# The first half of a merge gate by seven products, with v computed early and gates parked in DRAM

## The chip, the cores and the metric

The kernel runs on one core of one Trainium2 chip, in one launch. The metric is the device time of one execution in microseconds (us). The kernel before was run three times: 893.97, 894.41 and 895.62 us, median 894.41.

The engines go by these names: PE multiplies matrices (PEld is its weight load), DVE and ACT work on tiles elementwise, POOL and SP here issue transfers (DMAs) and do little else. Weights come from DRAM (also called HBM); SBUF is the on-chip memory for operands, PSUM the one that PE writes to.

## The reference

One encoder block over 256 tokens of width 2048. All inputs of the two branches, their gates and the two merge gates come out of one projection `z`; `m_lru` and `m_attn` are the merge gates' 2048 columns each.

```python
xn = rms_norm(x, norm_pre_w[l])
z = xn @ w_in[l]
u_lru, g_lru, q, k, v, g_attn, m_lru, m_attn = jnp.split(z, split_at, axis=-1)
u = centred_depthwise_conv(u_lru, conv_w[l], conv_b[l])
h = rg_lru(u, ..., False) + rg_lru(u, ..., True)
y_a = h.astype(x.dtype) * jax.nn.silu(g_lru)
...
y_b = windowed_gqa(q, k, v, attn_sink[l]) * jax.nn.silu(g_attn)
merged = (jax.nn.sigmoid(m_lru) * (y_a @ w_proj_a[l])
          + jax.nn.sigmoid(m_attn) * (y_b @ w_proj_b[l]))
x = x + rms_norm(merged @ w_out[l], norm_post_w[l])
```

## The kernel before

**Weights.** Every weight matrix is read in cells of 1 MB (128 x 2048 float32), in the order that `load_plan` writes down; two fetches of half a MB make up some of them. A cell's two halves are split by `split` (L231, L233) into a high part `wh` (rounded by ACT's cast) and a low part `wl` (what is left, by DVE), and PE forms each product from three matrix products: high by high, low by high, high by low (`mm3`, L237 to L239; L262 and L264 do the same with the two parts of the activation side by side). There are three kinds of cells. A "blk" gives 128 output columns with the weights as the stationary side (`add_pair`: the gates `gl` and `ga`, the recurrent inputs `u`, the keys `k`, the queries `q`). A "quad" is a quarter of 512 output columns with tokens as the stationary side (`add_rows`: `ml`, `v_ps`, `pa`, `ma`, `pb`, `o`); four quads make a chunk. A "part" is half of one of seven products (below).

**Seven products.** Half of a merge gate (1024 columns) can be had from seven products of half-size blocks in place of eight, in `Seven`: two token blocks by two halves of the inner dimension by two column halves of 512. The products m1 to m7 use sums of weight blocks and of activation blocks. The weight sums are formed by the transfers: a block is loaded by SP (`start`), and others are added to it in SBUF by accumulating DMAs that POOL issues (`load` with `add`, L204). The activation sums are formed by DVE (`x_sums`), stored to DRAM by SP (`away`) and fetched back a half product at a time (`x_sum`, L349). Each product has two parts, of 12 matmuls each, where a quad has 24. The results are put together by DVE (`combine`, L756) from PSUM and copies that ACT made (`keep`, L425). Before the change `Seven("L")` computes columns 1024 to 2047 of `m_lru`, `Seven("A")` the same columns of `m_attn`, and `Seven("O")` half of the output projection. Columns 0 to 1023 of `m_lru` are two chunks of quads, `ml0` and `ml1`, by `add_ml`.

**Order of the work.** The emission loop at the end of `body` walks over the cells in ticks. A tick is one half of a blk or quad, or a whole part: 12 matmuls of 512 columns, or 8 of 512 and 8 of 256. In each tick the loop issues a fetch three cells ahead (sums and chained loads four and five ahead), runs the closures due at that tick, has ACT cast the weights four halves ahead and DVE form the low part three halves ahead, and then emits PE's matmuls. Every engine works through its own queue in this order. Closures are put at a tick by `at`, `soon` and `behind`: the recurrence of a pair of blocks (`lru_pair`, from tick `LRU[c]`), the heads of attention, the evacuations of PSUM. The program has 298 ticks. The first 142, up to v's last, are:

- `u` quads (ticks 0 to 7), `ml0` (8 to 15), then gl, ga and u pairs, `ml1` at ticks 40 to 47, and between the blks from tick 56 to 121 the 14 parts of `L`, one after every second blk (`EARLY_L`);
- the keys, and v's four quads at ticks 134 to 141.

Then `MERGE` takes over: queries and the projections `pa` in turn, the gate `m_attn` with its seven products, `pb`, and at last the output projection.

**Buffers.** Tiles of 4 KB a partition come from one pool of 45 (`unit`); raw cells go through a ring of three; PSUM has four single banks (`bank`) and two double ones. Of the values that wait long, the chunks 0 and 1 of the merge gate and the products `pa` of chunks 2 and 3 are stored to DRAM by `park` (L780) and fetched by `back` (L783), all on SP's queue. The silu gates `sgl` and `sga` stay in SBUF, and `ya`, the recurrent branch's result in two parts, is made as soon as a pair's recurrence ends (`y_parts`).

Of the kernel before, what the change touches and what calls it, by code (L numbers as in the profile page):

```python
# [27 lines left out]
ROT = 32  # L28
EPS = 1e-6
UNITS = 45  # L30
EARLY = (0, 2)
DECAY = 12
SPIN = 10
HEAD0 = 5
FIRST = 8
ROWS = 10
U0, GL0, Q0, K0, V0, GA0, ML0, MA0 = 0, 2048, 4096, 6144, 6656, 7168, 9216, 11264
# [28 lines left out]
CHUNKS = {"p": ("w_proj_a", 0), "a": ("w_in", MA0), "b": ("w_proj_b", 0), "o": ("w_out", 0)}  # L66
SEVENS = {"L": ("w_in", ML0 + 1024), "A": ("w_in", MA0 + 1024), "O": ("w_out", 0)}


PV_NORM = 0  # L70
# [9 lines left out]
def load_plan():  # L80

    plan = []

    def quad(m, c):
        plan.extend(("quad", m, c, i) for i in range(4))

    def pair(m, c, n):
        plan.extend(("blk", m, c + (n + i) * P, 0) for i in range(2))

    quad("w_in", U0)  # L90
    for i in range(8):
        if i in EARLY:
            quad("w_in", ML0 + EARLY.index(i) * 512)
        for j, c in enumerate([GL0 + 2 * i * P, GA0 + 2 * i * P] + [U0 + (2 * i + 4) * P] * (i < 6)):
            for n in range(2):
                plan.append(("blk", "w_in", c + n * P, 0))
                if (i, 2 * j + n) in EARLY_L:
                    a, q = EARLY_L[i, 2 * j + n].split(".")
                    plan.append(("part", "L", a, int(q)))
    pair("w_in", K0, 0)  # L100
    pair("w_in", K0, 2)
    quad("w_in", V0)
    for o in MERGE + OUT:
        a, i = o.split(".")
        if a[0] in SEVENS:
            plan.append(("part", a[0], a[1:], int(i)))
        elif a[0] == "q":
            plan.append(("blk", "w_in", Q0 + (4 * int(a[1]) + int(i)) * P, 0))
        else:
            w, c = CHUNKS[a[0]]  # L110
            plan.append(("quad", w, c + int(a[1]) * 512, int(i)))
    return plan


# [13 lines left out]
def body(ctx, tc, x, xT, wall, wlru, pvec, npost, ident_d, mask_d, rope_d, out):  # L128
# [442 lines left out]
    for g in range(4):  # L571
        steps.append(("quad", lambda h, wh, wl, g=g: u_quad(g, h, wh, wl)))

    upads = {}

# [58 lines left out]
    def lru_pair(n, b):  # L634
# [69 lines left out]
        def gate_out():  # L704
# [13 lines left out]
        for d, fn in (  # L718
            (0, lambda: conv(0)), (1, lambda: conv(1)), (2, weights), (3, u_parts),
            (6, lambda: gates(0)), (7, lambda: sigmoids(0)), (8, lambda: gates(1)), (9, lambda: sigmoids(1)),  # L720
            (10, lambda: decays("th", AF.Tanh, cpos, 0)), (10, lambda: decays("th", AF.Tanh, cpos, 1)), (11, gated),
            (12, lambda: decays("a", AF.Exp, cneg, 0)), (13, lambda: decays("a", AF.Exp, cneg, 1)),
            (13, lambda: nc.scalar.activation(v["gr"], v["a"], AF.Square)), (14, scale1),
            (15, lambda: nc.scalar.activation(v["th"], v["th"], AF.Sqrt)),
            (19, lambda: nc.vector.tensor_tensor(v["gi"], v["gi"], v["th"], ALU.mult)),
            (21, lambda: scans(0)), (24, lambda: scans(1)), (28, gate_out), (29, y_parts),
        ):
            at(b + d, fn)

    def silu_evac(units_list, n):  # L730
# [16 lines left out]
    def gate_unit(gates, c):  # L747
        if c not in gates:
            gates[c] = unit(f"mg{c}", F32, (P, 2, 512))
        return gates[c]  # L750

    def gate_evac(gates, c):
        return lambda t, ps: nc.scalar.activation(gate_unit(gates, c)[:, t], ps, AF.Sigmoid, scale=rtok[:, t:t + 1])

    def combine(to, ps, other, sign):
        nc.vector.scalar_tensor_tensor(to, ps, float(sign), other, ALU.mult, ALU.add if sign > 0 else ALU.subtract)  # L756

    def gate_sum(gates):

        def done(t, c, ps, other, sign):  # L760
            to = gate_unit(gates, 2 + c)[:, t]
            gate = lambda src: nc.scalar.activation(to, src, AF.Sigmoid, scale=rtok[:, t:t + 1])
# [12 lines left out]
    parked = {}  # L775

    def park(gates, c):

        d = parked[c] = dram.tile([P, 1024], F32, name=f"park{c}")
        nc.sync.dma_start(d, flat(gates.pop(c)))  # L780

    def back(gates, c):
        nc.sync.dma_start(flat(gate_unit(gates, c)), parked[c])  # L783
# [9 lines left out]
    for c in range(8):  # L793
        if c in EARLY:
            add_ml(EARLY.index(c))
        first_step = len(steps)
        add_pair(f"gl{2 * c}", xs, silu_evac(sgl, 2 * c))
        add_pair(f"ga{2 * c}", xs, silu_evac(sga, 2 * c))
        if c < 6:
            n = 2 * c + 4  # L800
            add_pair(f"u{n}", xs, lambda ps, n=n: scaled(upad_tile(n)[:, :, 2:2 + S], ps))
        mine = steps[first_step:]
        del steps[first_step:]
        for j, s in enumerate(mine):
            steps.append(s)
            if (c, j) in EARLY_L:
                a, q = EARLY_L[c, j].split(".")
                groups["L"].add(a, int(q))
        lru_pair(2 * c, LRU[c])


    swap = [(i + 16) % 32 for i in range(32)]
# [5 lines left out]
        nc.sync.dma_start(table["mask"], mask_d)  # L818
        nc.sync.dma_start(table["rope"], rope_d)

    at(ticks() - 6, load_tables)

    def add_heads(name, then):

# [27 lines left out]
                then(v["h"], v["l"])  # L852
                v.clear()

        for n in (0, 2):
            add_pair(f"{name}{n}", xs, evac(n))

    kv = {}
    add_heads("k", lambda h, l: kv.update(kh=h, kl=l))

    def v_evac(t, ps):
        if t == 0:
            kv["vh"], kv["vl"] = (unit(f"v{s}", F32R, (P, 2, 512)) for s in "hl")
        vh, vl = kv["vh"][:, t], kv["vl"][:, t]
        nc.scalar.activation(vh, ps, AF.Copy, scale=rtok[:, t:t + 1])
        soon(lambda: nc.vector.scalar_tensor_tensor(vl, ps, rtok[:, t:t + 1], vh.bitcast(F32), ALU.mult, ALU.subtract))

    add_rows("v_ps", xs, v_evac)

    def head(hd, qh, ql, b, both):  # L870

# [50 lines left out]
        def gate_out():  # L922
            y = sga[g][:, j - 1:j + 1]
            nc.vector.tensor_tensor(y, both["o"], y, ALU.mult)
            both.clear()

        for d, fn in ((0, scores), (1, expo), (3, normalise), (5, flip), (6, p_parts)):
            at(b + d, fn)
# [9 lines left out]
    def heads(g):  # L938
        def then(h, l):
            b = now[0] + HEAD0  # L940
            for j in range(4):
                if j % 2 == 0:
                    both = {}
                head(4 * g + j, h, l, b + 4 * j, both)
        return then


    def add_pa(c):
        def done(t, ps):
            nc.vector.tensor_tensor(tm[c][:, t], ps, tm[c][:, t], ALU.mult)  # L950
            if t == 1 and c >= 2:
                soon(lambda: park(tm, c), 2)

        add_rows(f"pa{c}_", ya, done)

# [23 lines left out]
    def add_all(order, classic):  # L979
        left, tick = {}, {}  # L980
        for o in order:
            a, i = o.split(".")
            tick[o] = ticks()
            if a[0] in SEVENS:
                groups[a[0]].add(a[1:], int(i))
                continue
            if i == "0":
                n = len(steps)
                classic(a[0], int(a[1]))
# [6 lines left out]
    tick = add_all(MERGE, lambda kind, c: {  # L996
        "q": lambda: add_heads(f"q{c}", heads(c)),
        "p": lambda: add_pa(c),
        "a": lambda: add_rows(f"ma{c}_", xs, gate_evac(sm, c)),
        "b": lambda: add_pb(c),  # L1000
    }[kind]())
    for c in range(4):
# [182 lines left out]
```

## Time and profile before

| what | value |
|---|---|
| median of three runs | 894.41 us |
| span of the profiled execution | 892.7 us |
| PE busy | 883.7 us (99%), 4590 matmuls |
| DVE busy | 698.5 us (78%), 959 instructions |
| ACT busy | 600.4 us (67%), 870 instructions |
| POOL busy | 44.8 us (5%), 72 instructions |
| DMA | 209.95 MB, mean 235 GB/s |
| HBM read, written | 200.78 MB, 8.39 MB |

The profiled execution's own time is its span of 892.7 us plus what lies around it; the median of the runs is 1.7 us above the span. Busy time is the union of an engine's instructions. Matmuls overlap in the pipeline and their ends are modelled, so that what a matmul costs in a saturated stream is the distance from its start to the next one's start, not its duration.

### The profile page before, as it was taken

Reading aid. Unit: us, or ns where it says so; the run is one execution under the profiler, and the core shown is the slowest. Engines: PE = TensorE matmul, PEld = TensorE weight load, DVE = VectorE, ACT = ScalarE, POOL = GpSimd, SP = SyncE. Lnnn points to the kernel's source line nnn. Section 1 sums busy time; section 2 is a strip of 40 time slices with the busy share of each in tenths; the row PEclk is TensorE's granted clock in tenths of the full one; section 3 lists DMA queues with packets and bytes.
Section 4 is the critical chain, followed back from the end, with each engine's and each line's share of the span. In section 5 each row is a group of like instructions: output and inputs, shape, how many; then the busy total and the mean of one; then the engine's idle time right before and its main releaser. Section 6 shows DMA issues by size and latency. Waiting matters only on the chain.

```text
span 892.7 us, 12161 instructions
## 1 busy us (share of the span) xinstructions
PE 883.7 (99%) x4590; PEld 758.2 (85%) x4590; DVE 698.5 (78%) x959; ACT 600.4 (67%) x870; POOL 44.8 (5%) x72
## 2 busy tenths in 40 slices
PE   9999999999999999999999999999999999999996
PEld 8888888888888888888888888888888888888885
DVE  6897999788888989899757767676676776687775
ACT  7689686787878788885454565455587654455754
POOL 0000000000110100000000000000101100000200
PEclk9999999999999999999999999999999999999998
DMA  9766667897797946365555444546979987799962
GB/s 337 260 224 237 211 226 281 245 297 280 242 303 259 276 172 217 107 230 198 211 185 213 162 168 145 209 146 239 280 253 310 286 258 256 278 325 378 232 177 95
DMA packets 43642, 209.95 MB, mean 235 GB/s; under 512 B 4512, under 2 KB 9376, under 8 KB 26560
## 3 DMA queue, kind: packets, MB, share of 16 engines
q1 hardware_dynamic: 36096, 183.25, 56.2%
q0 software_dynamic: 6912, 25.17, 14.9%
q8 instruction: 36, 0.59, 0.3%
q10 hardware_dynamic: 576, 0.76, 0.2%
q14 instruction: 22, 0.18, 0.1%
HBM read 200.78 MB, written 8.39 MB: 234 GB/s over the span
## 4 chain that ended last, share of the span: by engine, by line
PE 93%; issue 4%; DMA 2%; DVE 0%; POOLq 0%; ACTq 0%; POOL 0%; DVEq 0%
PE q L264 7%; PE gl L264 7%; PE ga L264 7%; PE u L264 5%; PE ga L262 3%; PE gl L262 3%; PE q L262 3%; PE u L262 3%; PE k L264 2%; PE Am L237 1%; PE Am L239 1%; PE Am L238 1%; PE Lm L239 1%; PE Lm L238 1%; PE Lm L237 1%
## 5 line engine op out<-in xcount | busy, mean ns | idle before, releaser
L233 DVE TENSOR_TENSOR wl<-raw,wh 128x1024 fp32r<-128x1024 f32 (+1 forms) x276 | 326.8, 1203 | 63.8 <-ACT wh L231 43.4
L231 ACT CAST wh<-raw 128x1024 fp32r<-128x1024 f32 (+1 forms) x275 | 275.8, 1040 | 43.5 <-DMA raw<-wall_dram 24.4
L264 PE MATMUL q<-xs,wh 128*128 128x512 f32 x256 | 62.8, 391 | 0.0
L264 PE MATMUL ga<-xs,wh 128*128 128x512 f32 x256 | 62.6, 391 | 0.0
L264 PE MATMUL gl<-xs,wh 128*128 128x512 f32 x256 | 62.6, 391 | 0.0
L264 PEld LDWEIGHTS ga<-xs,wh 128*128 128x128 f32 x256 | 46.9, 188 | 9.0
L264 PEld LDWEIGHTS gl<-xs,wh 128*128 128x128 f32 x256 | 46.9, 188 | 9.0
L264 PEld LDWEIGHTS q<-xs,wh 128*128 128x128 f32 x256 | 46.6, 188 | 8.8
L264 PE MATMUL u<-xs,wh 128*128 128x512 f32 x192 | 46.9, 391 | 0.0
L160 ACT CAST ph<-pt 128x512 fp32r<-128x512 f32 x16 | 9.4, 588 | 55.3 <-PE pt L908 55.3
L264 PEld LDWEIGHTS u<-xs,wh 128*128 128x128 f32 x192 | 35.0, 188 | 6.6
L262 PE MATMUL q<-xs,wl 128*128 128x256 f32 x256 | 34.4, 284 | 0.0
L262 PEld LDWEIGHTS ga<-xs,wl 128*128 128x128 f32 x256 | 33.2, 191 | 1.3
L262 PEld LDWEIGHTS q<-xs,wl 128*128 128x128 f32 x256 | 33.1, 191 | 1.2
L262 PE MATMUL ga<-xs,wl 128*128 128x256 f32 x256 | 34.0, 283 | 0.0
L262 PEld LDWEIGHTS gl<-xs,wl 128*128 128x128 f32 x256 | 32.9, 191 | 1.2
L262 PE MATMUL gl<-xs,wl 128*128 128x256 f32 x256 | 33.4, 283 | 0.0
L888 DVE CUSTOM_DVE_ANT_0 p<-sc,table,pv 128x256 f32<-128x256 f32 x32 | 16.1, 541 | 13.4 <-PE sc L239 13.4
L262 PEld LDWEIGHTS u<-xs,wl 128*128 128x128 f32 x192 | 24.6, 191 | 0.9
L262 PE MATMUL u<-xs,wl 128*128 128x256 f32 x192 | 24.9, 283 | 0.0
L658 DVE SCALAR_TENSOR_TENSOR uu<-upad,pv,uu 128x256 f32<-128x256 f32 x48 | 23.2, 483 | 2.2 <-ACT uu L654 0.5
L681 ACT ACTIVATE gr<-gate,pv 128x256 f32<-128x256 f32 x32 | 15.2, 476 | 11.7 <-PE gate L239 11.7
(493 smaller groups left out, 2188.5 us busy)
## 6 DMA issues: line engine op xcount, KB each, us to landing
raw<-wall_dram SPq DMA_DIRECT2D x133, 1024.0 KB, 5.8
lraw<-wlru_dram SPq DMA_DIRECT2D x8, 512.0 KB, 7.0
away<-xx SPq DMA_DIRECT2D x8, 512.0 KB, 4.5
Lm<-away SPq DMA_DIRECT2D x8, 512.0 KB, 7.9
Am<-away SPq DMA_DIRECT2D x8, 512.0 KB, 8.0
raw<-wall_dram SPq DMA_DIRECT2D x8, 256.0 KB, 5.2
park<-mg SPq DMA_DIRECT2D x4, 512.0 KB, 6.1
mg<-park SPq DMA_DIRECT2D x4, 512.0 KB, 6.2
```

Source lines behind the costliest of these rows:

```text
L160: nc.scalar.copy(h, src)
L231: cast(hs, raw)
L233: nc.vector.tensor_tensor(ls, raw, hs.bitcast(F32), ALU.subtract)
L237: nc.tensor.matmul(ps, wh, xh, start=start, stop=False, skip_group_check=more)
L238: nc.tensor.matmul(ps, wh, xl, start=False, stop=False, skip_group_check=more)
L239: nc.tensor.matmul(ps, wl, xh, start=False, stop=stop, skip_group_check=more)
L262: nc.tensor.matmul(ps[:, 1], wl[:, sl], a[:, 0], start=False, stop=False)
L264: nc.tensor.matmul(ps, wh[:, sl], a, start=k == 0, stop=k == KT - 1)
L658: nc.vector.scalar_tensor_tensor(u, up[:, j, tap:tap + S], cw[:, tap:tap + 1], u, ALU.mult, ALU.add)
L681: nc.scalar.activation(v["gr"][:, 2 * d + j], ps[:, 0], AF.Sigmoid, bias=pv[:, PV_BR + b:PV_BR + b + 1])
L888: nc.vector.tensor_tensor_reduce(p[:, t], sc[:, t], table["mask"][:, t], rtok_sc[:, t:t + 1], sk, ALU.add, ALU.max, m[:, t:t + 1])
```

## The change

The two chunks `ml0` and `ml1` are gone. A further object `Seven("M")` computes columns 0 to 1023 of `m_lru` by seven products, its 14 parts standing behind those of `L`. v's four quads take the place of `ml0` right after `u`; the keys stand at the end, between M's last parts. The order up to the keys is now written out in a table, `START`, which `load_plan` and `add_all` both read. The parts of `L` begin earlier, at tick 44, one behind each blk for the most part, those of M follow from tick 92 to 137; the eight `x_sums` stand every four ticks from tick 18 on, where they stood every five from 20. The pairs' recurrences start at ticks 12, 28, 42, 58, 75, 92, 109 and 122, where they started at 12, 28, 45, 64, 79, 94, 109 and 121. The program has 296 ticks; `p0.0`, the first projection cell, is at tick 148 in place of 150.

More values are kept in DRAM: the gates `sgl` (three of four tiles, once multiplied with the recurrence's result), `sga` (all four tiles, and three of them again once multiplied with the attention's result), all four chunks of the gate, and all four products `pa`. That makes 18 parks and 18 returns of 512 KB each, where there were four and four. Six of the eight `ya` are therefore formed later, in ticks 145 to 151, from the fetched tiles.

The core of the diff:

```diff
-EARLY = (0, 2)
...
-EARLY_L = {(2, 3): "m1.0", (2, 5): "m1.1", (3, 1): "m2.0", (3, 3): "m2.1", (3, 5): "m5.0", (4, 1): "m5.1", (4, 3): "m3.0",
-           (4, 5): "m3.1", (5, 1): "m6.0", (5, 3): "m6.1", (5, 5): "m7.0", (6, 1): "m7.1", (6, 3): "m4.0", (7, 1): "m4.1"}
-XSUM = (20, 25, 30, 35, 40, 45, 50, 55)
-LRU = (12, 28, 45, 64, 79, 94, 109, 121)
...
+START = """u0.0 u0.1 u0.2 u0.3 v0.0 v0.1 v0.2 v0.3 g0.0 g0.1 h0.0 h0.1 w4.0 w4.1 g2.0 g2.1 h2.0 h2.1 w6.0 w6.1 g4.0 g4.1
...
+XSUM = (18, 22, 26, 30, 34, 38, 42, 46)
+LRU = (-4, 0, 2, 2, 2, 2, 2, 4)
...
+SEVENS = {"L": ("w_in", ML0 + 1024), "M": ("w_in", ML0), "A": ("w_in", MA0 + 1024), "O": ("w_out", 0)}
...
-        def y_parts():
-            q = n // 2
-            ya[q] = pair_unit(f"ya{q}")
-            parts_of(ya[q][:, :, 0], ya[q][:, :, 1], sgl[n // 4][:, n % 4:n % 4 + 2])
+            if n in (2, 6, 10):
+                soon(lambda: park("ya", sgl, n // 4), 2)
+            elif n > 10:
+                soon(lambda: y_parts(n // 2))
...
+                if units_list is sga and n % 4 == 2:
+                    soon(lambda: park("sga", sga, n // 4), 3)
...
     Seven("L", xs, None, gate_sum(tm))
+    Seven("M", xs, None, gate_sum(tm, 0))
...
-    def add_ml(c):
-        def done(t, ps):
-            gate_evac(tm, c)(t, ps)
-            if t == 1:
-                soon(lambda: park(tm, c), 2)
-
-        add_rows(f"ml{c}_", xs, done, c == 0)
...
+    def park(key, store, c):
+
+        d = parked[key, c] = dram.tile([P, 1024], F32, name=f"park{key}{c}")
+        t = store[c]
+        store[c] = None
+        nc.sync.dma_start(d, flat(t))
+
+    def back(key, store, c, shape=(P, 2, 512)):
+        store[c] = unit(f"{key}{c}", F32, shape)
+        nc.sync.dma_start(flat(store[c]), parked[key, c])
...
     for c in range(4):
-        at(tick[f"p{c}.0" if c < 2 else f"b{c}.0"], lambda c=c: back(tm, c))
+        at(tick[f"p{c}.0"], lambda c=c: back("tm", tm, c))
+        at(tick[f"b{c}.0"], lambda c=c: back("pa", tm, c))
+    for c in range(4):
+        if c < 3:
+            at(tick["p0.0"] - 8 + 2 * c, lambda c=c: back("ya", sgl, c, (P, 4, S)))
+            at(tick["b0.0"] - 12 + 3 * c, lambda c=c: back("yb", sga, c, (P, 4, S)))
     for n in range(8):
-        at(tick["b0.0"] - 4 + 3 * n // 2, lambda n=n: yb_parts(n))
+        if n < 6:
+            at(tick["p0.0"] - 3 + n, lambda n=n: y_parts(n))
+        at(tick["b0.0"] - 6 + 3 * n // 2, lambda n=n: yb_parts(n))
```

In `START` g and h stand for pairs of the gates `gl` and `ga`, w for pairs of `u`, and `Lm1.0` for the first part of L's product m1. Its M stretch, from the first part to the last of M, reads: `Mm1.0 g10.1 Mm1.1 h10.0 h10.1 Mm2.0 w14.0 Mm2.1 w14.1 Mm5.0 g12.0 Mm5.1 g12.1 Mm3.0 h12.0 h12.1 Mm3.1 g14.0 Mm6.0 g14.1 Mm6.1 h14.0 Mm7.0 h14.1 Mm7.1 k0.0 k0.1 Mm4.0 k2.0 Mm4.1`.

**Three places in the order.** First PE, where `u` ends and the next chunk begins (tick 8). Before, the first chunk of the gate:

```order
L554 MATMUL u_ps_195<-xs_263,wh_1_290 128x512 x2
L554 MATMUL u_ps_196<-xs_263,wh_1_290 128x512 x2
L237 MATMUL ml_0_409<-wh_0_315,xs_124 128x512
L238 MATMUL ml_0_409<-wl_0_316,xs_124 128x512
L239 MATMUL ml_0_409<-wh_0_315,xs_124 128x512
```

After, v stands there with the same shapes, and the gate's columns come on PE as parts between two halves of a blk (tick 92, the first of them):

```order
L250 MATMUL gl_2784<-xs_258,wh_1_2725 128x512 x2
L250 MATMUL gl_2784<-xs_263,wh_1_2725 128x512 x2
L223 MATMUL Mm_2831<-wh_0_2756,xs_124 128x512
L224 MATMUL Mm_2831<-wl_0_2757,xs_124 128x512
L225 MATMUL Mm_2831<-wh_0_2756,xs_124 128x512
L223 MATMUL Mm_2831<-wh_0_2756,xs_135 128x512
```

What moved: 192 matmuls of `ml` are replaced by 168 of `Mm`, and v's 96 stand 126 ticks earlier.

Second DVE, just before the first `pa` chunk, where the first queries' rotation (`q0f`, `q0s`), the last recurrence (`gr`) and the low parts of weights (`wl`) are in the queue. Before:

```order
L589 TENSOR_TENSOR q0f_4229<-q_4144,q0f_4229 128x512
L233 TENSOR_TENSOR wl_0_4232<-raw_4183,wh_0_4231 128x1024
L841 STREAM_SHUFFLE q0s_4275<-q0f_4229 32x512
L842 TENSOR_TENSOR q0f_4229<-q0f_4229,table 32x512
L233 TENSOR_TENSOR wl_1_4254<-raw_4183,wh_1_4253 128x1024
L707 TENSOR_TENSOR gr_3794<-gr_3794 128x512
L708 TENSOR_TENSOR sg_3301<-gr_3794,sg_3301 128x512
L845 TENSOR_TENSOR q0s_4275<-q0s_4275,table 32x512
L846 TENSOR_TENSOR q0f_4229<-q0f_4229,q0s_4275 32x512
L233 TENSOR_TENSOR wl_0_4279<-raw_4227,wh_0_4278 128x1024
L233 TENSOR_TENSOR wl_1_4303<-raw_4227,wh_1_4302 128x1024
L161 TENSOR_TENSOR ya_4324<-sg_3301,ya_4324 128x2x256
```

After (`ya_4195` and `ya_4247` on the right of an arrow are the tiles fetched from DRAM):

```order
L147 TENSOR_TENSOR ya_4324<-ya_4195,ya_4324 128x2x256
L219 TENSOR_TENSOR wl_1_4329<-raw_4245,wh_1_4328 128x1024
L826 TENSOR_TENSOR q0s_4354<-q0s_4354,table 32x512
L827 TENSOR_TENSOR q0f_4301<-q0f_4301,q0s_4354 32x512
L147 TENSOR_TENSOR ya_4352<-ya_4195,ya_4352 128x2x256
L219 TENSOR_TENSOR wl_0_4359<-raw_4296,wh_0_4358 128x1024
L147 TENSOR_TENSOR ya_4378<-ya_4247,ya_4378 128x2x256
L219 TENSOR_TENSOR wl_1_4384<-raw_4296,wh_1_4383 128x1024
L147 TENSOR_TENSOR ya_4407<-ya_4247,ya_4407 128x2x256
L147 TENSOR_TENSOR q0l<-q0f_4301,q0h 128x512
L576 TENSOR_TENSOR q0f_4413<-q_4307,q0f_4413 128x512
L219 TENSOR_TENSOR wl_0_4416<-raw_4348,wh_0_4415 128x1024
```

What moved: six `ya`, which stood singly between ticks 42 and 124, now stand one in each tick ahead of the chunk that reads them, the low part two ticks ahead of PE's use.

Third SP, where it fetches for the last third of the recurrences' weights (`lraw`; `raw` is a cell, `Lm` an activation sum). Before:

```order
L219 DMA raw_2678<-wall_dram 128x2048
L349 DMA Lm_2680<-away_74 128x1024
L640 DMA lraw_2710<-wlru_dram 128x1024
L219 DMA raw_2759<-wall_dram 128x2048
L219 DMA raw_2814<-wall_dram 128x2048
L349 DMA Lm_2816<-away_75 128x1024
L219 DMA raw_2893<-wall_dram 128x2048
L219 DMA raw_2947<-wall_dram 128x2048
L349 DMA Lm_2949<-away_74 128x1024
```

After, around the same fetch of `lraw`:

```order
L192 DMA Mx0a<-wall_dram 128x1024
L192 DMA Mx0b<-wall_dram 128x1024
L787 DMA parktm_2696<-mg_2403 128x1024
L627 DMA lraw_2721<-wlru_dram 128x1024
L787 DMA parkya_2723<-sg_1453 128x1024
L205 DMA raw_2745<-wall_dram 128x2048
L192 DMA Mx1a<-wall_dram 128x1024
L192 DMA Mx1b<-wall_dram 128x1024
L205 DMA raw_2821<-wall_dram 128x2048
L787 DMA parktm_2825<-mg_1814 128x1024
L205 DMA raw_2848<-wall_dram 128x2048
L205 DMA raw_2901<-wall_dram 128x2048
```

What moved: M's first weight blocks and three parks stand among the raw cells; in the whole program SP issues 268 transfers in place of 230, POOL 64 accumulating ones in place of 48.

More of the change, by code (lines that the diff above doesn't have):

```diff
@@ L34 @@
 HEAD0 = 5
+STRIDE = 4
 FIRST = 8
@@ L82, in load_plan @@
     plan = []
[L84 to L103, printed above, removed]
+    for o in START + MERGE + OUT:
         a, i = o.split(".")
@@ L106, in load_plan @@
             plan.append(("part", a[0], a[1:], int(i)))
-        elif a[0] == "q":
-            plan.append(("blk", "w_in", Q0 + (4 * int(a[1]) + int(i)) * P, 0))
-        else:
-            w, c = CHUNKS[a[0]]
-            plan.append(("quad", w, c + int(a[1]) * 512, int(i)))
+        elif a[0] in PAIRS:
+            n = int(a[1:]) * (4 if a[0] == "q" else 1) + int(i)
+            plan.append(("blk", "w_in", PAIRS[a[0]] + n * P, 0))
+        else:
+            w, c = QUADS[a[0]]
+            plan.append(("quad", w, c + int(a[1:]) * 512, int(i)))
     return plan
@@ L569, in u_quad, with add_u @@
                         product(wh, j, b, k, a, slice(0, 2), slice(0, 2), k == KT - 1)
-    for g in range(4):
-        steps.append(("quad", lambda h, wh, wl, g=g: u_quad(g, h, wh, wl)))
+    def add_u():
+        for g in range(4):
+            steps.append(("quad", lambda h, wh, wl, g=g: u_quad(g, h, wh, wl)))
     upads = {}
@@ L725, in lru_pair, with y_parts @@
             (19, lambda: nc.vector.tensor_tensor(v["gi"], v["gi"], v["th"], ALU.mult)),
-            (21, lambda: scans(0)), (24, lambda: scans(1)), (28, gate_out), (29, y_parts),
+            (21, lambda: scans(0)), (24, lambda: scans(1)), (28, gate_out),
         ):
             at(b + d, fn)
+    def y_parts(q):
+        ya[q] = pair_unit(f"ya{q}")
+        n = q % 2 * 2
+        parts_of(ya[q][:, :, 0], ya[q][:, :, 1], sgl[q // 2][:, n:n + 2])
     def silu_evac(units_list, n):
@@ L750, in gate_unit, with gated_out, done, gate_sum @@
         return gates[c]
+    def gated_out(gates, c, t):
+        if t == 1 and gates is tm:
+            soon(lambda: park("tm", tm, c), 2)
     def gate_evac(gates, c):
-        return lambda t, ps: nc.scalar.activation(gate_unit(gates, c)[:, t], ps, AF.Sigmoid, scale=rtok[:, t:t + 1])
+        def done(t, ps):
+            nc.scalar.activation(gate_unit(gates, c)[:, t], ps, AF.Sigmoid, scale=rtok[:, t:t + 1])
+            gated_out(gates, c, t)
+        return done
     def combine(to, ps, other, sign):
         nc.vector.scalar_tensor_tensor(to, ps, float(sign), other, ALU.mult, ALU.add if sign > 0 else ALU.subtract)
-    def gate_sum(gates):
+    def gate_sum(gates, first=2):
         def done(t, c, ps, other, sign):
-            to = gate_unit(gates, 2 + c)[:, t]
-            gate = lambda src: nc.scalar.activation(to, src, AF.Sigmoid, scale=rtok[:, t:t + 1])
+            to = gate_unit(gates, first + c)[:, t]
+            def gate(src):
+                nc.scalar.activation(to, src, AF.Sigmoid, scale=rtok[:, t:t + 1])
+                gated_out(gates, first + c, t)
             if other is None:
@@ L775, in body @@
     parked = {}
[L777 to L783, printed above, removed]
-    def add_ml(c):
-        def done(t, ps):
-            gate_evac(tm, c)(t, ps)
-            if t == 1:
-                soon(lambda: park(tm, c), 2)
-        add_rows(f"ml{c}_", xs, done, c == 0)
[L793 to L809, printed above, removed]
+    def park(key, store, c):
[6 more added lines that the diff above has]
+        nc.sync.dma_start(flat(store[c]), parked[key, c])
     swap = [(i + 16) % 32 for i in range(32)]
@@ L819, in load_tables @@
         nc.sync.dma_start(table["rope"], rope_d)
-    at(ticks() - 6, load_tables)
     def add_heads(name, then):
@@ L853, in rotate @@
                 v.clear()
-        for n in (0, 2):
-            add_pair(f"{name}{n}", xs, evac(n))
+        return lambda n: add_pair(f"{name}{n}", xs, evac(n))
     kv = {}
-    add_heads("k", lambda h, l: kv.update(kh=h, kl=l))
     def v_evac(t, ps):
@@ L925, in gate_out @@
             both.clear()
+            if j == 3 and g < 3:
+                soon(lambda: park("yb", sga, g), 2)
         for d, fn in ((0, scores), (1, expo), (3, normalise), (5, flip), (6, p_parts)):
@@ L940, in then @@
             b = now[0] + HEAD0
+            soon(lambda: back("sga", sga, g, (P, 4, S)), HEAD0 + 4)
             for j in range(4):
@@ L943, in then @@
                     both = {}
-                head(4 * g + j, h, l, b + 4 * j, both)
+                head(4 * g + j, h, l, b + STRIDE * j, both)
         return then
@@ L950, in done @@
             nc.vector.tensor_tensor(tm[c][:, t], ps, tm[c][:, t], ALU.mult)
-            if t == 1 and c >= 2:
-                soon(lambda: park(tm, c), 2)
+            if t == 1:
+                soon(lambda: park("pa", tm, c), 2)
         add_rows(f"pa{c}_", ya, done)
@@ L995, in body, with add_q @@
     seven = Seven("O", ms, msum, lambda *a: o_sum(*a))
-    tick = add_all(MERGE, lambda kind, c: {
-        "q": lambda: add_heads(f"q{c}", heads(c)),
+    heads_k = add_heads("k", lambda h, l: kv.update(kh=h, kl=l))
+    def add_q(c):
+        pair = add_heads(f"q{c}", heads(c))
+        for n in (0, 2):
+            pair(n)
+    silu_of = {"g": (sgl, "gl"), "h": (sga, "ga")}
+    silu_pair = lambda kind, n: add_pair(f"{silu_of[kind][1]}{n}", xs, silu_evac(silu_of[kind][0], n))
+    tick = add_all(START + MERGE, lambda kind, c: {
+        "u": add_u,
+        "g": lambda: silu_pair("g", c),
+        "h": lambda: silu_pair("h", c),
+        "w": lambda: add_pair(f"u{c}", xs, lambda ps: scaled(upad_tile(c)[:, :, 2:2 + S], ps)),
+        "k": lambda: heads_k(c),
+        "v": lambda: add_rows("v_ps", xs, v_evac, True),
+        "q": lambda: add_q(c),
         "p": lambda: add_pa(c),
@@ L1001, in body @@
     }[kind]())
+    for c in range(8):
+        lru_pair(2 * c, tick[f"g{2 * c}.0"] + LRU[c])
+    at(tick["k0.0"] - 6, load_tables)
     for c in range(4):
-        at(tick[f"p{c}.0" if c < 2 else f"b{c}.0"], lambda c=c: back(tm, c))
+        at(tick[f"p{c}.0"], lambda c=c: back("tm", tm, c))
[4 more added lines that the diff above has]
+            at(tick["b0.0"] - 12 + 3 * c, lambda c=c: back("yb", sga, c, (P, 4, S)))
     for n in range(8):
-        at(tick["b0.0"] - 4 + 3 * n // 2, lambda n=n: yb_parts(n))
+        if n < 6:
+            at(tick["p0.0"] - 3 + n, lambda n=n: y_parts(n))
+        at(tick["b0.0"] - 6 + 3 * n // 2, lambda n=n: yb_parts(n))
     npt, xr, yw = [], [[], []], [[], []]
```

12 lines of the change are left out of this document (8 added, 4 removed).

## The prediction

> **What bounds the kernel now.** I read the page first: shares, slices, chain.
>
> ```profile
> span 892.7 us, 12161 instructions
> PE 883.7 (99%) x4590; PEld 758.2 (85%) x4590; DVE 698.5 (78%) x959; ACT 600.4 (67%) x870; POOL 44.8 (5%) x72
> ...
> PE   9999999999999999999999999999999999999996
> ...
> DVE  6897999788888989899757767676676776687775
> ...
> PEclk9999999999999999999999999999999999999998
> ...
> PE 93%; issue 4%; DMA 2%; DVE 0%; POOLq 0%; ACTq 0%; POOL 0%; DVEq 0%
> ```
>
> PE is busy in every slice at full clock and carries the chain. DVE is second, at nine tenths in the first half, where the change lies. A busy PE may still wait inside a modelled matmul, so next its waits, over the whole run:
>
> ```profile
> engine line waited for: us in total, times, longest us
> PE spin L458 <- POOL eps L454: 1.0, 1, 1.0
> ```
>
> One wait, at the very start. So time is PE's list of matmuls plus a fixed head and tail: what leaves the list is gained, whatever lets PE wait is lost, and relief elsewhere is worth nothing. What one matmul costs I take from PE's timeline, by starts: the second gate chunk `ml1` begins at the first row, and the next blk at the second.
>
> ```profile
> 124.23 0.39 PE L237 MATMUL ml__1324<-wh,xs 128*128 128x512 f32 x1
> ...
> 145.99 0.39 PE L264 MATMUL gl<-xs,wh 128*128 128x512 f32 x1
> ```
>
> 96 matmuls in 145.99 - 124.23 = 21.76 us: 0.2267 us each (not the 0.39 of one row, which is its latency).
>
> **PE's part of the change.** Two chunks of 96 go (192, 43.52 us); 14 parts of 12 come (168, 38.08 us). Everything else on PE keeps its count; v only moves, its shapes being those of `ml`. The saving is 24 x 0.2267 = 5.44 us. More can't be had, since PE waits for nothing that the change could shorten. The rest of the working asks whether PE stays fed.
>
> **DVE and ACT up to the keys' end.** Busy times of the stretch that answers to ticks 16 to 141, of ticks 120 to 151, and of `q0` and `p0`:
>
> ```profile
> 51.60:423.00 371.40, 371.40 (x2087) 326.22 (x2086) 325.40 (x417) 293.87 (x410) 14.99 (x28) 1.00 0.72 238
> ...
> 360.00:451.00 91.00, 91.00 (x493) 79.13 (x492) 77.53 (x99) 62.56 (x82) 0.00 (x0) 1.00 0.54 191
> ...
> 423.00:468.00 45.00, 45.00 (x230) 38.52 (x229) 29.67 (x37) 23.16 (x27) 0.00 (x0) 1.00 0.56 199
> ```
>
> (columns: stretch, length, then busy us of PE, PEld, DVE, ACT, POOL). What one added instruction costs:
>
> ```profile
> L233 DVE TENSOR_TENSOR wl<-raw,wh x276: 685/1219/1227, 6.0 to 875.6; 128x1024 fp32r<-128x1024 f32 x134, 128x512 fp32r<-128x512 f32 x4
> L231 ACT CAST wh<-raw x275: 602/1051/1081, 7.0 to 873.3; 128x1024 fp32r<-128x1024 f32 x134, 128x512 fp32r<-128x512 f32 x4
> ...
> L425 ACT COPY Lm<-Lm x2: 581/582/582, 188.8 to 246.4; 128x512 f32<-128x512 f32 x2
> L756 DVE SCALAR_TENSOR_TENSOR mg<-Lm,Lm x2: 683/684/686, 218.4 to 338.0; 128x512 f32<-128x512 f32 x2
> ...
> L161 DVE TENSOR_TENSOR ya<-sg,ya 128x512 fp32r<-128x512 f32 x8 | 5.5, 682 | 0.0
> L866 DVE SCALAR_TENSOR_TENSOR vl<-v_ps,rtok,vh x2: 742/746/751, 425.1 to 425.8; 128x512 fp32r<-128x512 f32 x2
> ```
>
> Eight quads have 16 halves to split, 14 parts have 28. DVE: 12 x 1.219 = 14.6 us; three combines like L's at 0.684 = 2.1; six `ya` leave the stretch, 6 x 0.682 = 4.1. Sum 325.4 + 12.6 = 338.0 of 371.4 - 5.4 = 366.0: idle shrinks from 46.0 to 28.0 us. ACT: 12 x 1.051 = 12.6, three copies 1.7, the gate's four sigmoids as before, six `ya` casts less: about 305 of 366. Both still fit, and the activation sums are the same eight, merely closer. The `ya` land in the next row, where DVE has 15 us to spare. Cost on PE: nothing, while low parts come in time.
>
> The spare there is small in places. DVE's row is the low part of the second half of the first blk of keys, PE's the matmuls that read it first:
>
> ```profile
> 377.10 1.22 DVE L233 TENSOR_TENSOR wl<-raw,wh 128x1024 fp32r<-128x1024 f32 x1
> ...
> 380.89 1.12 PE L262 MATMUL k<-xs,wl 128*128 128x256 f32 x8
> ```
>
> 380.89 - 378.32 = 2.6 us. In ticks 120 to 151, the place around it, the new order gives DVE five more low parts (6.1 us), four `ya` net (2.7), two combines (1.4), and five rotation and silu products of 0.68 that slide in against v's two of 0.746 (1.9): 77.5 + 12.1 = 89.6 of 91.0 us. That is nearly full. Lower bound of the cost: 0, if the 13.5 us of idle time can all be used. Upper bound: 12.1 - 2.6 = 9.5 us of PE waiting, if none can. I take 0 to 0.5, being nearest to the row of 371.4 us, where DVE is 88% busy and PE waits nowhere; and the later stretch (66%) takes over what is left.
>
> **Transfers.** By the order: six MB more of gate weights (14 against 8), eight more activation sums and 28 more parks and returns of half a MB, 24 MB in all, on a mean of 235 GB/s.
>
> ```profile
> q1 hardware_dynamic: 36096, 183.25, 56.2%
> q0 software_dynamic: 6912, 25.17, 14.9%
> ...
> raw<-wall_dram SPq DMA_DIRECT2D x133, 1024.0 KB, 5.8
> ...
> Lx1b<-wall_dram POOLq DMA_DIRECT2D x3, 512.0 KB, 11.2
> ```
>
> A plain MB takes 0.562 x 892.7 / 183.25 = 2.74 us of the DMA engines, an accumulated one 0.149 x 892.7 / 25.17 = 5.28. Eight ticks last 892.7 x 8 / 298 = 24.0 us. The fullest eight after the change are 208 to 215: 7.34 MB plain and 2.10 added, 20.1 + 11.1 = 31.2 us, 7.2 too many; the next eight have 17.2 and clear it. Before, ticks 280 to 287 hold 3.15 and 4.19 MB, 30.8 us, 6.8 too many, and PE did not wait there. So 0, with 7.2 us less whatever lead there is as the upper end. An add is issued five cells ahead and cast two ahead, three cells or five ticks of 21.76 / 8 = 2.72, so 13.6 us, against a landing of 11.2; that lead is the same for one part per blk as for one per two.
>
> SP issues 38 more at 0.33 us (12.5 us) and idles 559 us for low parts alone. A park waits for its value two ticks back, and the raw cells queue behind it. Parks before waited 7.9 us at worst, with no PE wait behind; I cost them at 0, covered by the raw cell's three cells of lead.
>
> ```profile
> SPq L219 <- DVE wl L233: 559.0, 113, 14.9
> ...
> SPq L780 <- DVE mg L950: 7.9, 1, 7.9
> ...
> L204 POOL DMA_DIRECT2D Lx1b<-wall_dram x3: 874/891/1233, 184.2 to 299.7; - x3
> ```
>
> **POOL** issues 16 more adds of 0.9 us each and is idle beside them: 0. The Trainium skill speaks against such adds: "GPSIMD Engine Reference", section 8, has GpSimd share its SBUF interfaces with VectorE, contended by DVE instructions with two SBUF inputs, which the low parts are. By that rule each add would hold DVE for 0.9 us, 14 us more, leaving 14 of its 28 idle; a pair of adds would take 1.8 of the 2.6 us of spare, so 889.0 would still stand unless two pairs fell together (3.6 - 2.6, one us each time). The trace hardly bears it out: low parts never exceed 1227 ns against a median of 1219, with 48 adds among them, while the longest add above took 1233 ns.
>
> **Sum.** 892.7 - 5.4 = 887.3 us of span. The median of the runs stands 1.7 us above the profiled span, which I leave as it is: 894.4 - 5.4 = 889.0 us.
>
> **The rivals.**
> 1. DVE falls behind by a little in several spots among the parts, where recurrences and two-split ticks meet. For it: nine tenths in the DVE slices, 2.6 us of spare. Against it: no PE wait today. Two or three waits of one us give 891 to 892.
> 2. Slower: DVE becomes the bound in ticks 120 to 151, 89.6 of 91.0 us. With the upper bound of 9.5 us it ends at 889.0 + 9.5 = 898.5. For it: the six `ya` have only two ticks (2 x 2.72 = 5.4 us) from their place in the queue to PE's use. Against it: a light stretch behind, and 13.5 us idle in it today. It decides from a lag of 2.6 + 5.4 = 8.0 us.
> 3. Transfers come late in the fullest places (three of them, around ticks 72, 127 and 215 to 240). With 2 us of PE waiting at each the gain is eaten: 889.0 + 6 = 895.0, no change. Against it: the 6.8 us of before that cost nothing.
>
> **How the numbers follow.** The forecast, 889.0, gets 0.70 (its own range 888.0 to 890.2), rival 1 0.13, rival 2 0.10, rival 3 0.07. No change can be told from one of 0.2% (1.8 us; the three runs alone spread by 1.65). Faster is the forecast and rival 1: 0.83; same is rival 3 with its neighbours: 0.06; slower, rival 2 and the worst of 3: 0.11. For 8 in 10 the range takes the forecast and rival 1: 887.8, a little under the full saving for the spread of runs, to 892.5.
>
> **What would show it.** Right: 4566 matmuls on PE, a single wait at the start, a span near 887.3, low parts ended before their matmuls around the keys, DVE idle about 28 us between v's and the keys' end. Wrong: PE waits for `wl` or `ya` by DVE near 360 to 450 us (rival 2) or spread over 130 to 360 us (rival 1); ACT waiting for raw cells or accumulated ones, and PE behind it, near 200, 360 and 640 us (rival 3). What I can't see before is how the bursts line up; a PE wait in the order of 8 us would turn the sign.

## The result, and the profile after

The changed kernel takes 894.18 us (median of 12 runs, 893.27 to 895.98); the kernel before, on the same chip, 894.13 us (12 runs). The ratio is 1.0001, 95% interval 0.9992 to 1.0009: no difference, where 889.0 was forecast and 892.5 was the upper end. The profiled execution took 894.17 us, its span is 892.2 us. It shows first that the work did shrink. The page of the changed kernel, with its shares, slices, DMA row, the chain and the median landing time of a raw cell (the last number of its row):

```profile
span 892.2 us, 12273 instructions
PE 879.0 (99%) x4566; PEld 753.0 (84%) x4566; DVE 714.1 (80%) x974; ACT 611.6 (69%) x885; POOL 58.6 (7%) x88
...
PE   9999999999899999999999999999999999999996
...
DVE  6899999898697987898987768576676776687776
...
DMA packets 51420, 235.13 MB, mean 264 GB/s; under 512 B 5377, under 2 KB 10241, under 8 KB 35105
...
PE 72%; DVE 9%; DMA 9%; issue 5%; ACT 3%; POOLq 0%; ACTq 0%; SPq 0%; DVEq 0%; POOL 0%
...
raw<-wall_dram SPq DMA_DIRECT2D x127, 1024.0 KB, 6.4
```

PE has 4566 matmuls, 24 fewer, and 4.7 us less busy time, yet the span is only 0.5 us shorter. The eleventh slice of PE (223 to 245 us) is no longer full, and the chain, 93% PE before, is 72% PE now and runs in part through DVE and DMA (9% each). Next, what PE waited for, over the whole run:

```profile
PE gl L250 <- ACT wh L217: 2.3, 1, 2.3
PE ga L248 <- DVE wl L219: 1.3, 2, 1.1
PE spin L444 <- POOL eps L440: 1.0, 1, 1.0
PE gate L223 <- ACT gi L669: 0.6, 1, 0.6
PE u_ps L540 <- DVE wh L217: 0.5, 1, 0.5
PE u_ps L540 <- DVE xs L471: 0.2, 1, 0.2
```

The `spin` row stood there before; the others are new. The two `u_ps` rows lie in the first 20 us, and such rows come and go among the runs below. Measured by starts against 0.2267 us (512 columns) and 0.119 us (256), PE lost 4.57 us between 225 and 250 us and 0.88 us between 350 and 375 us, 5.45 in all: the whole saving of 5.44, most of it in one place. What released it there is in the chain, cut to 205 to 232 us:

```profile
189.62 15.86 DMA raw<-wall_dram
...
208.98 0.70 DVE sg L730
209.67 0.02 issue
209.69 0.33 SPq L787
...
210.11 20.62 DMA raw<-wall_dram
230.73 0.02 issue
230.75 1.05 ACT wh L217
231.80 0.04 issue
231.85 0.50 PE gl L250
```

A raw cell of the gate `gl` is issued at 210.11 us, takes 20.62 us to land, is cast at once, and PE starts on it at 231.85. Over the run the median raw cell lands in 6.4 us. Ahead of it in the chain is SP issuing a park (L787) as soon as DVE has its value. So there are two candidates, slow transfers and SP's queue. Transfers and queue are seen in these stretches, of before and then of after (the last columns are the clock, the DMA share, and GB/s):

```profile
164.00:174.00 10.00, 10.00 (x53) 8.59 (x52) 8.26 (x12) 7.11 (x12) 0.49 (x1) 1.00 0.96 261
180.00:246.00 66.00, 66.00 (x371) 57.92 (x370) 55.38 (x66) 53.83 (x72) 4.78 (x10) 1.00 0.82 270
```

```profile
164.00:174.00 10.00, 10.00 (x57) 8.73 (x56) 5.93 (x7) 9.61 (x12) 0.87 (x1) 1.00 0.72 293
...
180.00:246.00 66.00, 62.45 (x344) 53.87 (x343) 53.54 (x63) 47.90 (x65) 8.98 (x14) 1.00 0.99 302
```

From 180 to 246 us the DMA engines have nothing to spare (0.99, against 0.82 before). Just ahead of that they idle for a quarter of ten microseconds. SP's timeline and SP's waits from 150 to 180 us tell why:

```profile
161.01 0.39 SPq L335 DMA_DIRECT2D Lm<-away  x1
164.06 0.33 SPq L205 DMA_DIRECT2D raw<-wall_dram  x1
173.08 0.33 SPq L787 DMA_DIRECT2D parkya<-sg  x1
173.50 0.41 SPq L205 DMA_DIRECT2D raw<-wall_dram  x1
173.97 1.45 SPq L192 DMA_DIRECT2D Ly0a<-wall_dram  x1
```

```profile
SPq L787 <- DVE sg L695: 8.7, 1, 8.7
```

SP stood 8.7 us for the value of the first parked branch result, which DVE's `gate_out` (L695) finished just before 173.08. A raw cell and the loads of L's `y` cells were behind it.

### The profile page after: what moved, and what is told of

It reads as the page before. It is cut to its first block, busy times and chain, and to the rows that moved or that the text cites. A ratio compares the mean times of both kernels' runs of the same rounds, so it can differ in the third digit from the quotient of the medians.

```text
span 892.2 us, 12273 instructions
## 1 busy us (share of the span) xinstructions
PE 879.0 (99%) x4566; PEld 753.0 (84%) x4566; DVE 714.1 (80%) x974; ACT 611.6 (69%) x885; POOL 58.6 (7%) x88
## 4 chain that ended last, share of the span: by engine, by line
PE 72%; DVE 9%; DMA 9%; issue 5%; ACT 3%; POOLq 0%; ACTq 0%; SPq 0%; DVEq 0%; POOL 0%
DMA raw<-wall_dram 9%; PE q L250 7%; DVE wl L219 5%; PE q L248 3%; PE ga L250 3%; PE gl L250 3%; PE k L250 2%; PE u L250 2%; PE ga L248 2%; ACT wh L217 2%; PE gl L248 2%; PE Am L225 1%; PE Am L223 1%; PE Am L224 1%; PE u_ps L540 1%
## 5 line engine op out<-in xcount | busy, mean ns | idle before, releaser
L219 DVE TENSOR_TENSOR wl<-raw,wh 128x1024 fp32r<-128x1024 f32 (+1 forms) x264 | 311.7, 1201 | 49.1 <-ACT wh L217 42.7
L217 ACT CAST wh<-raw 128x1024 fp32r<-128x1024 f32 (+1 forms) x263 | 264.7, 1037 | 57.6 <-DMA raw<-wall_dram 44.5
L250 PEld LDWEIGHTS gl<-xs,wh 128*128 128x128 f32 x256 | 46.9, 188 | 11.7 <-ACT wh L217 2.7
L146 ACT CAST ms<-mt 128x512 fp32r<-128x512 f32 x8 | 4.7, 588 | 24.2 <-PE mt L950 24.2
## 6 DMA issues: line engine op xcount, KB each, us to landing
Lm<-away SPq DMA_DIRECT2D x8, 512.0 KB, 16.9
```

The source lines that it names most:

```text
L146: nc.scalar.copy(h, src)
L217: cast(hs, raw)
L219: nc.vector.tensor_tensor(ls, raw, hs.bitcast(F32), ALU.subtract)
L250: nc.tensor.matmul(ps, wh[:, sl], a, start=k == 0, stop=k == KT - 1)
```

## The experiments

Three theories at first. **A**: the transfer work alone is too much for the stretch of L's parts (rival 3 of the prediction). **B**: SP's queue, in order, holds the raw cells back behind parks. **C**: DVE is full and makes the low parts late (rivals 1 and 2).

**Adds made plain.** The eight added loads of L overwrite the cell; what is left out is said in the expectation.

```diff
-                nc.gpsimd.dma_start(flat(cell[h]), w[:, h * 1024:(h + 1) * 1024], accum_op=ALU.add)
+                x = dict(accum_op=ALU.add) if p[1] != "L" else {}
+                nc.gpsimd.dma_start(flat(cell[h]), w[:, h * 1024:(h + 1) * 1024], **x)
```

> The eight weight loads that are added to L's cells (8 MB) become plain loads in the same place of the same queue; the sums of L's weight blocks are left out of the computation, every instruction of PE, DVE and ACT stays. At 5.28 us of the DMA engines for an added MB and 2.74 for a plain one this takes 20 us of transfer work out of 150 to 245 us. Theory A (the DMA engines' time is the limit there): the PE waits near 229 to 245 us (4.6 us) go, the one near 354 us (0.8 us, M's own adds) stays, about 889.6 us. Theory B (SP's queue, in order, issues raw cells late behind parks and activation sums): same queue, so about 894. Theory C (DVE is full and makes the low parts late): same DVE work, so about 894.

Measured: 888.86 us, ratio 0.9939 (0.9922 to 0.9956). That is the curing which A forecast, with no PE wait left but those of the first 20 us; the one near 354 us, which A let stand, is gone too. DVE's work is the same, so C falls. But the windows and SP's waits of this run (here L788) say more:

```profile
164.00:174.00 10.00, 10.00 (x58) 8.77 (x57) 6.07 (x7) 8.52 (x12) 0.53 (x1) 1.00 0.71 283
...
180.00:246.00 66.00, 66.00 (x369) 57.80 (x368) 60.44 (x72) 52.20 (x73) 5.61 (x14) 1.00 0.83 318
```

```profile
SPq L788 <- DVE sg L696: 8.5, 1, 8.5
```

SP stands 8.5 us here too, and the DMA engines idle as before (0.71), but it costs nothing: later they have room (0.83) to catch up.

**Two parks later, all parks from ACT, and another order**, beside it:

```diff
-                soon(lambda: park("ya", sgl, n // 4), 2)
+                soon(lambda: park("ya", sgl, n // 4), 2 if n > 2 else 26)
...
-                    soon(lambda: park("sga", sga, n // 4), 3)
+                    soon(lambda: park("sga", sga, n // 4), 3 if n != 6 else 21)
```

> Two of the eleven parks move out of the crowded stretch: the first of the branch results by 24 ticks, the second of the attention silu gates by 18 ticks; nothing is left out. Theory A: 1 MB, 2.7 us of transfer work, leaves the queue, and the PE waits near 229 to 245 us shrink by 1 to 2.7 us: 891.5 to 893. Theory B: the two waits of SP on DVE's results go too, and raw cells are issued on time: about 889.6. Theory C: 894.

```diff
-        nc.sync.dma_start(d, flat(t))
+        nc.scalar.dma_start(d, flat(t))
```

> All parks are issued from ACT's queue instead of SP's; nothing is left out, the bytes and their times are the same. Theory A: same bytes, so within 1 us of 894. Theory B: nothing of DVE's or ACT's results stands in SP's queue, raw cells are issued early, the waits near 229 to 245 us go: about 890. If ACT loses time by waiting on DVE for the parks, it is slower than 894.

Measured: parks later 889.97 us, 0.9951 (0.9936 to 0.9965); parks from ACT 889.43 us, 0.9946 (0.9931 to 0.9961). In both the waits between 225 and 250 us are gone. That is B's number, not A's: the second run moves the same bytes in the same stretch (0.99 busy from 180 to 246 us), and is 4.7 us faster than the changed kernel. One rule of the Trainium skill would have said that this run gains little: "DMA: Bandwidth & Descriptors", section "Issuing engines are not separate DMA queues", has DMAs of all issuers share the same 16 engines, so that a second issuer saves only the time to initiate them. The runs differ: to initiate a park takes 0.33 us in the rows above, and moving a single one (below) gains 3.6 us, since what is saved is the standing of a queue. The stretches of the run with all parks from ACT:

```profile
164.00:174.00 10.00, 10.00 (x53) 8.58 (x52) 6.72 (x8) 9.83 (x13) 0.88 (x1) 1.00 1.02 419
...
180.00:246.00 66.00, 66.00 (x369) 57.85 (x368) 59.42 (x71) 51.38 (x70) 9.00 (x14) 1.00 0.99 302
```

The other order puts L's m1 and m2 earlier and moves the rest of L's and M's parts apart:

```diff
-    Lm1.0 h4.0 h4.1 Lm1.1 w8.0 Lm2.0 w8.1 Lm2.1 g6.0 Lm5.0 g6.1 Lm5.1 h6.0 h6.1 Lm3.0 w10.0 Lm3.1 w10.1 Lm6.0 g8.0
...
-    Mm4.0 k2.0 Mm4.1 k2.1""".split()
+START = """u0.0 u0.1 u0.2 u0.3 v0.0 v0.1 v0.2 v0.3 g0.0 g0.1 h0.0 h0.1 w4.0 w4.1 g2.0 Lm1.0 g2.1 h2.0 Lm1.1 h2.1
...
+    Mm6.1 h14.0 h14.1 k0.0 Mm7.0 k0.1 k2.0 Mm7.1 Mm4.0 Mm4.1 k2.1""".split()
```

> The same parts, blks and transfers in another order up to the keys: L's m1 and m2 come earlier, two or three blks stand between parts that bring added weights, nothing is left out. Worked out with a queue of the transfers at 2.74 and 5.28 us a MB against ticks of 2.725 us, the latest raw cell is 3 us before its use where the changed kernel's is 6 us too late. Theory A: all PE waits but the one at the start go, 889.0. Theory B: the parks still stand in SP's queue, 891 to 894. Theory C: DVE has the same work in the same stretch, 894.

Measured: 896.57 us, ratio 1.0031 (1.002 to 1.0041), slower than both. A miss for every theory. The waits near 229 to 245 us are gone here too, but two new ones have come:

```profile
PE Mm L223 <- DVE mg L756: 3.7, 1, 3.7
...
PE gate L224 <- DVE ul L147: 0.9, 1, 0.9
```

The new order puts `Mm4.0` right behind `Mm7.1`, and m4 is summed in the PSUM bank that m7 leaves: PE waits at 408 us until DVE, behind the low parts and the keys' rotation, has combined m7. By starts it lost 6.8 us between 400 and 425 us, and 3.9 of them are the wait itself. Behind it the matmuls start 0.43 us apart in place of 0.227, up to 417.5 us, and the granted clock from 412 to 418 us is 0.51:

```profile
411.86 0.77 PE L223 MATMUL Mm<-wh,xs 128*128 128x512 f32 x1 [3.74 <-DVE mg L756]
412.43 0.63 PE L224 MATMUL Mm<-wl,xs 128*128 128x512 f32 x1
412.86 0.63 PE L225 MATMUL Mm<-wh,xs 128*128 128x512 f32 x1
```

The longest wait of the changed kernel, 2.3 us, has nothing of the kind behind it (clock 1.00). So rival 2's mechanism exists, in this order and not in the one predicted. As a test of A it says little, since SP's standing for the first park is gone in it too: the DMA share of 164 to 174 us is 1.04.

With A's run and B's run both fast, the theory that takes both in is **D**: SP's standing and the full DMA engines do it together. Before 180 us the standing idles the engines by (1.02 - 0.72) x 10 us = 3.0 us (1.02 is what they have there with all parks issued by ACT); after that there is no room to give it back. Four runs test D, of which the first two are complements:

```diff
-        nc.sync.dma_start(d, flat(t))
+        (nc.scalar if (key, c) == ("ya", 0) else nc.sync).dma_start(d, flat(t))
```

> One instruction changes its queue: the first park of a branch result (ya 0) is issued by ACT, the other ten parks stay on SP; bytes and work are the same. Theory D (the two together: SP stands 8.7 us for that park's value at 164 to 173 us while the transfer engines fall to 0.72 busy, and from 180 us they are full and can't give it back): the DMA share of 164 to 174 us goes from 0.72 to about 1.0, the PE waits of 229 to 245 us go, the one near 354 us (0.8 us) stays: 889.5 to 890.2. Theory A (the transfer work alone): 894.

```diff
-        nc.sync.dma_start(d, flat(t))
+        (nc.sync if (key, c) == ("ya", 0) else nc.scalar).dma_start(d, flat(t))
```

> The complement: ten parks are issued by ACT, the first park of a branch result alone stays on SP. Theory D: SP stands there as before, the waits of 229 to 245 us (4.6 us) stay, the one near 354 us goes: 893 to 893.6. Theory B in its wide form (every park costs a little): only a tenth of the loss stays, about 890.

```diff
-                soon(lambda: park("ya", sgl, n // 4), 2)
+                soon(lambda: park("ya", sgl, n // 4), 6 if n == 2 else 2)
```

> The same park stays in SP's queue but stands four ticks later in it, behind the two loads of L's y cells and their activation sums, when its value has long been there; it is still in the crowded stretch, so the bytes there are the same. Theory D: as with ACT issuing it, 889.5 to 890.2. Theory A: same transfer work in the same stretch, 894.

```diff
-                soon(lambda: park("ya", sgl, n // 4), 2)
+                soon(lambda: park("ya", sgl, n // 4), 6)
...
-                    soon(lambda: park("sga", sga, n // 4), 3)
+                    soon(lambda: park("sga", sga, n // 4), 7)
...
-            soon(lambda: park("tm", tm, c), 2)
+            soon(lambda: park("tm", tm, c), 6)
...
-                soon(lambda: park("yb", sga, g), 2)
+                soon(lambda: park("yb", sga, g), 4)
...
-                soon(lambda: park("pa", tm, c), 2)
+                soon(lambda: park("pa", tm, c), 4)
```

> All parks of gates and branch results up to the keys stand four ticks later in SP's queue, those behind the keys two ticks; nothing is left out. Theory D: SP stands for none of them, both PE waits go: 888.7 to 889.3. If the units they free are missed four ticks longer, loads wait for a unit instead and it stays above 890.

| run | us, median | ratio to before | PE waits at 225 to 250 us |
|---|---|---|---|
| changed kernel | 894.18 | 0.9992 to 1.0009 | 4.6 us |
| that park alone from ACT | 890.63 | 0.9945 to 0.9974 | none |
| all parks but that one from ACT | 893.00 | 0.9975 to 0.9993 | 3.9 us |
| that park four ticks later | 891.57 | 0.9953 to 0.9979 | 1.8 us |
| all parks later | 889.17 | 0.9925 to 0.9954 | none |

(waits by starts). One half-megabyte store out of 18 parks (the expectations count the eleven up to the keys) decides: issued elsewhere, the waits of the place are gone, with all others on SP; left alone on SP, 3.9 of 4.6 us stay. The stretch of 164 to 174 us in the first and the second of the four runs:

```profile
164.00:174.00 10.00, 10.00 (x57) 8.73 (x55) 6.90 (x7) 9.56 (x12) 0.88 (x1) 1.00 1.02 409
```

```profile
164.00:174.00 10.00, 10.00 (x55) 8.65 (x54) 6.33 (x7) 9.79 (x13) 0.88 (x1) 1.00 0.76 305
```

The first came out 0.4 us above its upper bound and the third 1.4 us. In the third a wait of 1.6 us for `ul` (L147) near 244 us is left, in the same full stretch; its cause is open. The wait near 354 us, which D let stand in the first run, shrank to 0.2 us there (by starts), with the other parks still on SP: what makes it is open too.

Then the dose, a longer standing, and the best version (all parks later) once more:

```diff
-                soon(lambda: park("ya", sgl, n // 4), 2)
+                soon(lambda: park("ya", sgl, n // 4), 1 if n == 2 else 2)
```

> The park of the first branch result stands one tick earlier in SP's queue, so that one more raw cell stands behind it and SP stands some 11.5 us there instead of 8.7; nothing is left out, the transfers are the same. Theory D: about 2.8 us more of the transfer engines' time is lost ahead of the crowded stretch, and the raw cells that have no slack left bring it to PE nearly one for one: 896 to 897.5. If the loss comes from the crowd alone or from the park's bytes: 894.

> The kernel with all parks four ticks later (two behind the keys) once more, in more rounds, as the version that could replace both. Theory D: no PE wait but those of the first 20 us, 888.7 to 889.5, some 5 us under the kernel before.

The longer standing took 894.85 us, ratio 1.0006 (0.9997 to 1.0015). SP stood 11.9 us and the DMA share of 164 to 174 us fell to 0.53, as meant:

```profile
164.00:174.00 10.00, 10.00 (x54) 8.61 (x53) 6.79 (x8) 9.92 (x13) 0.87 (x1) 1.00 0.53 213
180.00:246.00 66.00, 63.56 (x349) 54.57 (x348) 53.34 (x62) 47.44 (x64) 8.98 (x14) 1.00 1.04 324
```

But the time rose by 0.7 us where 1.8 to 3.3 were expected, and this interval overlaps that of the changed kernel (0.9992 to 1.0009). By starts PE lost 1.4 us at 201 us, which is new, and 3.8 between 225 and 250. So the price isn't one for one: 0 us of standing to 8.7 cost 3.6 us (890.63 to 894.18), the next 3.2 about 0.7. In this run the share from 180 to 246 us is 1.04, in the changed kernel 0.99 with 0.91 from 228 to 244: the engines still had something to catch up with. That this makes the difference is argued, not shown. Nor is a standing ahead of full engines dear everywhere. In the changed kernel SP stood longer for two other parks:

```profile
SPq L787 <- ACT mg L764: 30.5, 3, 12.1
...
SPq L787 <- DVE tm L929: 12.6, 1, 12.6
```

The first (12.1 us) ended at 280 us, the second at 620, and the DMA share of the 16 us behind the first is 1.03, of 630 to 650 us 1.03 (mean of 1.05 and 1.01). PE waits nowhere near either. D is shown for the one place, not as a rule of how much a standing costs.

The best version took 889.13 us (5 runs, 888.84 to 889.22), ratio 0.9944 (0.993 to 0.9957): 5.0 of the 5.44 us, faster than both kernels. Its profile, waits of PE (one row) and the same two stretches:

```profile
PE spin L444 <- POOL eps L440: 1.0, 1, 1.0
```

```profile
164.00:174.00 10.00, 10.00 (x58) 8.77 (x58) 6.39 (x8) 9.47 (x12) 0.87 (x1) 1.00 1.01 401
180.00:246.00 66.00, 66.00 (x369) 57.84 (x368) 58.70 (x70) 50.45 (x68) 8.99 (x14) 1.00 0.99 299
```

The second stretch is as full as in the changed kernel. The raw cell that PE waited for there (landed 230.73, used 231.85) is issued at 208.68 here, cast at 223.20 and used at 229.19.

## Why the prediction was wrong

**PE's saving, right.** 4566 matmuls, and 5.0 to 5.3 us faster in the runs where nothing holds PE up (889.13 and 888.86 against 894.16).

**DVE and ACT, right.** DVE's busy time rose by 15.6 us (714.1 - 698.5; predicted 14.6 + 2.1 with the `ya` moved, not removed). For the stretch up to the keys' end the sum was too high: DVE was busy 329.9 of 371.4 us there (51.6 to 423.0), where 338.0 of 366.0 were forecast, so that it idled 41.5 us and not 28; which term was too large isn't known. From 360 to 451 us it was busy 85.6 us (89.6 forecast). Where ticks 120 to 151 and the keys were feared, PE waits nowhere between 375 us and the end of the keys. The new row for `wl` (1.3 us) lies at 242 to 245 us: DVE, which had idled 7.9 us up to 231.8 for the cell that came late, was then working off its queue.

**Adds on POOL, right.** The rule of the Trainium skill, "GPSIMD Engine Reference", section 8, as the prediction read it, would have each add hold a low part. With 64 adds instead of 48 the longest low part took 1228 ns against a median of 1218: the trace again doesn't bear it out.

**Transfers at 0, right by themselves, and just so.** The best version moves the same 24 MB more without a wait. But the fullest eight ticks weren't the place that counted: PE waited for nothing at ticks 208 to 215, and the lead was used up at ticks 76 and 79, a place that only rival 3 named. There the DMA engines were full for 48 us on end (1.03 to 1.05 in the three slices of 16 us from 180 to 228), where the working took eight ticks, 24 us, at a time. The median fetch of an activation sum of L there took 16.9 us, while the adds to L's `x` cells still landed in 9.8 to 11.7.

**Parks on SP at 0, wrong. This is the step that failed.** "Parks before waited 7.9 us at worst, with no PE wait behind; I cost them at 0, covered by the raw cell's three cells of lead." The size of the wait was forecast well (8.7 us here), its price was not: 3.6 us for this one park (894.18 against 890.63), and 5.0 in the best version (889.13), where SP stands for the parks no longer but for 0.7 us and, near 610 us, 9.6. Three cells of lead were there, but the term above it had already spent lead on the transfers' excess; the same lead was used twice. And the row of 7.9 us was from a stretch of the kernel before (L950, behind the keys), not from the one where the change made the transfers full. What a standing SP does to the DMA engines, idle time that must be made up, wasn't asked.

**The rivals.** Rival 3 had the place (around tick 72), the look (ACT waiting for raw cells, PE behind it) and nearly the time (895.0), by bytes alone, at three places of 2 us each. It was one place of 4.6 us and one of 0.9, and bytes alone did not do it: that its time is so near is in part luck. Rival 3 and the wait of a park stood in the prediction as separate items, each too small to matter; that the one could fall into the other's place was no rival at all.

## What to carry to other kernels

Before a wait on an in-order issuing queue is called covered, write down all that the same lead has to cover in that stretch, and add it up once. A store that waits for a late value shouldn't stand in the queue that feeds the bound engine: put it a few ticks later, or on a queue with nothing urgent behind it; here that is worth 5 us of 894. When two relieving experiments both cure a loss, look for a cause that needs both conditions, and test it by undoing a single instruction.

## What the hardware showed that was not expected

In the full stretch the excess didn't fall on all transfers alike. The DMA view of the changed kernel from 205 to 222 us:

```profile
q0 software_dynamic: 597, 2.17, 63.9%
q1 hardware_dynamic: 595, 2.70, 41.2%
...
raw<-wall_dram SPq DMA_DIRECT2D x3, 1024.0 KB, 20.6
...
Lx0b<-wall_dram POOLq DMA_DIRECT2D x1, 512.0 KB, 11.7
Lx1a<-wall_dram POOLq DMA_DIRECT2D x1, 512.0 KB, 9.8
```

The adds (q0) and SP's transfers (q1) got the same number of packets, 597 and 595. The adds' packets take longer, so q0 took 63.9% of the engines' time and its transfers landed about as fast as ever (11.2 us before), while the raw cells on q1 took three times their median of 6.4. That fits "DMA: Bandwidth & Descriptors" of the Trainium skill, section "Queues, rings and completion order": each engine takes turns between the queues that have work, a packet at a time. Here the queue that brings PE's raw cells bore the delay. In the same 17 us the second of the four runs, with 3.9 of the 4.6 us of loss, has 567 and 564 packets, the best version 622 and 526, so the counts are not equal in every run.
